# A four-layer decoder step on one core: cache copies issued from ScalarE, key and value tiles in another ring, and a scheduler with other DMA durations

## The chip, the cores and the metric

The kernel runs on one core of one Trainium2 chip. The core's engines are PE (TensorE), ACT (ScalarE), DVE (VectorE) and POOL (GpSimd), each with an instruction queue that is worked off in order, and SP (SyncE), whose queue here only starts transfers; the transfers of all queues run on the core's 16 DMA engines. The metric is the device time of one execution in microseconds; three runs of the kernel before gave 2403.86, 2408.07 and 2417.21 us.

## What is computed

The reference is one inference step of a trunk of four layers, for a prompt of 1024 tokens and a sample of 8 sequences with 4 tokens each. Layers are A (gated short convolution), B (native sparse attention), C (RG-LRU) and A again, each followed by a LayerNorm of `ALPHA * x + mixer(x)`. What bears on the change:

```
def short_conv_mixer(x, buf, w_in, conv_w, w_out):          # layers A
    h, b_gate, c_gate, z = jnp.split(x @ w_in, 4, axis=-1)
    conv, new_buf = causal_dwconv(c_gate * h, buf, conv_w)
    return (jax.nn.silu(z) * b_gate * conv) @ w_out, new_buf

def nsa_mixer(x, past_rows, win_buf, w_in, w_cmp, w_out):   # layer B
    kv = proj[..., D_ATT:D_ATT + n_kvcols].reshape(bsz, t_len, 6, N_KV, HEAD_DIM)
    rows, win_new = kv[:, :, :4], kv[:, :, 4:]
    full = jnp.concatenate([past_rows, rows], axis=1)        # past_rows: 4096 cached rows per sequence
    kv_c = jnp.einsum('bnjcgd,cjgd->bncgd', blocks, w_cmp)   # compressed keys and values, 32 rows to 1
    all_win = jnp.concatenate([win_buf, win_new], axis=1)
    return y, rows, all_win[:, all_win.shape[1] - keep:]     # the last 512 sliding-window rows
```

So the sliding-window output of the sample is, per sequence, rows 4 to 511 of the cached window (508 rows of 1 KB) followed by the 4 new rows: the first part is a plain copy from one DRAM tensor to another, with nothing computed.

## The kernel before

Activations lie feature by token: 8 tiles of 128 features by 1056 tokens (1024 of the prompt, 32 of the sample). A float32 value is kept as a rounded high part and a low remainder, and a product is three matmuls, so one **dense step** (`dense`, L629: one 128-feature output tile, 352 tokens) is 8 x 3 = 24 matmuls of 352 columns into one PSUM bank of the ring "mm" (5 banks). The text calls U[c] the c-th of the eight tiles, from the ring "big", that hold a mixer's output for the out projection.

**First layer** (`layer_a`, L952): 8 channels of 4 x 3 dense steps, 96 in all. For each channel, w = 0 gives h (copied to SBUF by ACT), w = 2 the gate product (DVE), w = 3 the SiLU factor (ACT, DVE), and w = 1 the convolution and the split into U[c] (DVE, ACT). Beside it runs layer B's **compression** of the cache (`compress`, L1296), 64 side steps: POOL gathers 1 MB of cached rows into a tile of "big", SP writes its selection half to the scratch tensor `raw` (two transfers of 256 KB), DVE or POOL multiplies the other half by weights (ring of one tile, reloaded from `in_b_w_cmp` every 8 steps), and DVE sums into one accumulator. Gather n waits for sum n - 3 (`GAHEAD`). Side steps are written out between the dense steps at a rate `RATE`, 0.7 per dense step (`share`, L610); the sums end in `kcd`.

**Out projection** (`out_phase`, L685): 24 dense steps that contract over all of U[0..7], LayerNorm in two rounds through DRAM (`dd`), new activations X.

**Layer B** (`b_project`, L1400): keys and values of 128 tokens at a time in two halves, in groups of four token tiles; each PSUM result is copied by ACT into a tile `kv` of the ring "c" (8 tiles), which also carries the tiles of the LayerNorm that is still running. Its rows are stored by SP, its keys transposed by PE and split by `put_k` (L1426), whose low part for g = 1 goes to DRAM (`kl1`). Then **decode** (`decode`, L1647) for the sample: 36 units of cached keys, fetched from `raw`; in between, `decode_select` for sequence pairs 1 to 3, begun at the units in `SELT`, reads `kcd` into a tile "sel". Then attention of the prompt (`prompt_attention`), with a plan of its own, the out projection, **layer C** (`layer_c`, L1084) and the **last layer** (`layer_a` again, without side steps) with `final_phase`.

**What sets the order.** All parts but the prompt's attention are recorded as steps and laid out by a planner (`Rec.lay`, L378): it simulates the five engines with costs per operation, takes the ready step with the earliest due time, and hands out the tiles of a ring in the order in which the program names them. A transfer costs SP 100 ns, its bytes run over one bus at 360 bytes per ns, and it lands 2000 ns later. The order so found is issued as it stands for four of the engines:

```
with self.tc.manual_schedule(engines={E.PE, E.Activation, E.DVE, E.Pool}):
```

SP is not among them (L485): its queue is ordered by the framework, by the data that a transfer depends on. The copy of the sliding-window rows is written in layer C (`gate_out`, L1189) with a planner's key `("z", c)`, which is no data; its source and destination are DRAM tensors that nothing else writes at these places:

```
nc.sync.dma_start(win_s[c, 0:508, :], cache[c, 4:512, :], rk=[("z", c)])
```

Of the kernel before, what the change touches and what calls it, by code (L numbers as in the profile page):

```python
# [240 lines left out]
class Rec:  # L241
# [136 lines left out]
    def lay(self):  # L378
# [9 lines left out]
        free = {e: 0.0 for e in self.ENGINES}  # L388
# [34 lines left out]
        order, bus, table = [], 0.0, None  # L423
        while True:
            best = None
            for e in self.ENGINES:
                if able[e]:
                    s = free[e]
                elif pend[e]:
                    s = max(free[e], pend[e][0][0])  # L430
# [6 lines left out]
            s, e = best  # L437
            while pend[e] and pend[e][0][0] <= s:
                _, i, o = heapq.heappop(pend[e])
                heapq.heappush(able[e], (o.due, i, o))  # L440
            o = heapq.heappop(able[e])[2]
# [6 lines left out]
            if e == "SP":  # L448
                free[e] = s + 100
                bus = max(bus, s + 100) + o.size / 360  # L450
                o.end = bus + 2000
            else:
                free[e] = o.end = s + cost
                if o.size:
                    bus = max(bus, o.end) + o.size / 360
                    o.end = bus + 2000
# [42 lines left out]
class Trunk:  # L499
# [452 lines left out]
    def layer_a(self, pm, a, X, lp, side=None, nxt=()):  # L952
        nc, io = self.nc, self.io
        stt = nc.vector.scalar_tensor_tensor
        win = io["a_w_in"][a]
        U = [None] * NCH
        SC = lp.tile([P, NCH, 36 if self.later else 18], F32, name="SC")
        todo = [(w, c) for c in range(NCH) for w in (0, 2, 3, 1)]
# [13 lines left out]
        for c in range(NCH):  # L972
            g = self.wsl(1074)
# [3 lines left out]
            W, hs, th = {}, {}, {}  # L977

            def step(w, j):
# [5 lines left out]
                ps = self.mm(pm)[:, 0:TC]  # L985
                self.dense(ps, W[w], X, j)
                if w == 0:
                    hs[j] = self.ct(TC)
                    nc.scalar.copy(hs[j], ps)
                elif w == 2:  # L990
# [8 lines left out]
                else:  # L999
# [4 lines left out]
                    o = j * TC  # L1004
# [79 lines left out]
    def layer_c(self, pm, X, lp):  # L1084
        nc, io = self.nc, self.io
# [103 lines left out]
        def gate_out(c):  # L1189
            h2, i = H[c // 2], c % 2  # L1190
            W = take(("z", c))
            u = self.view2(self.big(F32R))
            U[c] = u
            for j in range(3):
                sl = slice(j * TC, (j + 1) * TC)
                ps = self.mm(pm)[:, 0:TC]
                self.dense(ps, W, X, j)
                th = self.ct(TC)
                nc.scalar.activation(th, ps, AF.Tanh, scale=0.5)
                stt(out=th, in0=th, scalar=1.0, in1=ps, op0=ALU.add, op1=ALU.mult)  # L1200
                stt(out=th, in0=th, scalar=0.5, in1=h2[:, i, sl], op0=ALU.mult, op1=ALU.mult, wk=[("z", c)])
                self.split(u[:, 0, sl], u[:, 1, sl], th, "act", "pool")

            nc.sync.dma_start(win_s[c, 0:508, :], cache[c, 4:512, :], rk=[("z", c)])
        UC, GT, WA, H = {}, {}, {}, {}
        todo = []
        for x in ORDER_C.split():
            c = int(x[1])
# [9 lines left out]
        def take(key):  # L1218
# [5 lines left out]
            return self.pre.pop(key)  # L1224
        win_s = io["o_nsa_win_sample"][0].rearrange("b t c g d -> b t (c g d)")
        cache = io["cache_nsa_win"][0].rearrange("b t c g d -> b t (c g d)")
        for x in ORDER_C.split():
# [172 lines left out]
    def b_project(self, pm, X, bs, ds):  # L1400
# [25 lines left out]
        def put_k(br, ps, g0, n):  # L1426


            for g in range(2):
                kd = K[br]  # L1430
# [12 lines left out]
        for half in range(2):  # L1443
# [8 lines left out]
            for g4 in ((0, 1, 2) if half == 0 else (2, 0, 1)):  # L1452
                tts = range(4 * g4, min(4 * g4 + 4, 9))
                kn = []
                if half == 1 and g4 == 0:
                    side = self.decode_prepare(pm, q2, self.decode_gates(pm, GS, ds), KN, VN, ds)
                for tt in tts:
# [9 lines left out]
                    next(side, None)  # L1467
                    kv = self.ct(nw)
                    if half == 0:
# [763 lines left out]
OUTS = ((0, 0), (0, 1), (1, 0), (1, 1))  # L2233
RATE = 0.7
GAHEAD = 3
# [18 lines left out]
SEL0 = 1  # L2254
SELT = (3, 9, 18)
DSH = dict(sel=7.1, kin=-11.8, begin=-11.6, keys=2.2, score=-10.9, turn=30.4, pv=-26.1, vin=-88.9, first=-37.1, vals=-23.0,
# [191 lines left out]
```

## Time and profile before

| | |
|---|---|
| median of 3 runs | 2408.07 us (2403.86 to 2417.21) |
| profiled execution | 2407.38 us, of which the trace's span is 2405.1 us |
| PE busy | 2303.5 us of the span |
| DVE, ACT, POOL busy | 1573.5, 1197.4, 963.3 us |
| moved by DMA | 320.34 MB, mean 133 GB/s |
| mean granted clock of PE | 0.979 of full speed |

The profile is one execution. Its page gives busy time by engine and in 40 slices of the span; the windows give the same for any stretch, with the count of instructions, so that a stretch in which PE ran slowly shows by fewer matmuls. Waits are put down to the instruction whose semaphore came last. Most instructions carry the line of the recording helper (L310), so they are told apart by the tiles that they write and read: "mm<-x,w" is a dense step on activations, "mm<-big,w" one on U. SP's instructions show when a transfer is started, not when it lands.

### The profile page before, as it was taken

What the parts mean: (1) busy time and instruction counts of PE and PEld (TensorE: products, weight loads), DVE (VectorE), ACT (ScalarE), POOL (GpSimd) and SP (SyncE); (2) the same over time, 40 slices, a digit from 0 to 9 for tenths busy, and PEclk for the clock granted to TensorE, in tenths of its full rate; (3) what the DMA queues carried; (4) which work ended last, traced back from release to release, by engine and by line L of the source; (5) the groups of instructions that cost most, each with busy time, mean ns of one, the idle gap of its engine ahead of it and who ended that gap; (6) DMA issues with size and microseconds to landing.
All of it is one profiled execution on the core that took longest, in us unless ns stands there. A gap on an engine that the chain in (4) does not pass through costs nothing. (4 is left out here: it accounts for less than half of the span.)

```text
span 2405.1 us, 41388 instructions
## 1 busy us (share of the span) xinstructions
PE 2303.5 (96%) x14801; PEld 2233.7 (93%) x14801; DVE 1573.5 (65%) x3686; ACT 1197.4 (50%) x2753; POOL 963.3 (40%) x1070
## 2 busy tenths in 40 slices
PE   8999999897989989999999999999999999999996
PEld 8999998796888879999999998999999999999996
DVE  5776675565348876777777776798875753333336
ACT  3111121234438777888888883378873442222233
POOL 3454543313137855565555663233464320000230
PEclk9999999998999989999999999999999999999998
DMA  8999998438356751111111243341114321111012
GB/s 274 344 350 328 305 293 276 130 124 278 107 163 224 270 193 52 46 41 44 51 40 44 73 137 100 119 138 53 36 46 124 111 62 53 44 45 53 27 55 73
DMA packets 334642, 320.34 MB, mean 133 GB/s; under 512 B 19462, under 2 KB 301542, under 8 KB 324964
## 3 DMA queue, kind: packets, MB, share of 16 engines
q1 hardware_dynamic: 325220, 250.58, 33.9%
q0 software_dynamic: 9216, 67.11, 7.6%
q8 instruction: 117, 1.92, 0.3%
q14 instruction: 89, 0.73, 0.1%
HBM read 237.31 MB, written 84.48 MB: 134 GB/s over the span
## 5 line engine op out<-in xcount | busy, mean ns | idle before, releaser
L310 PE MATMUL mm<-x,w 128*128 128x352 f32 x5760 | 943.8, 325 | 19.0 <-DVE ws L310 10.5
L310 PEld LDWEIGHTS mm<-x,w 128*128 128x128 f32 x5760 | 933.4, 190 | 24.0 <-DVE ws L310 8.1
L310 PE MATMUL mm<-big,w 128*128 128x352 f32 x2208 | 379.5, 326 | 12.0 <-ACT big L310 9.6
L310 PEld LDWEIGHTS mm<-big,w 128*128 128x128 f32 x2208 | 358.0, 189 | 15.8 <-ACT big L310 9.9
L310 POOL TENSOR_TENSOR w<-ws,w 128x1024 fp32r<-128x1024 f32 (+1 forms) x43 | 105.9, 2462 | 419.2 <-ACT w L310 416.9
L1993 DVE TENSOR_TENSOR c<-T,c 128x512 fp32r<-128x512 f32 (+1 forms) x320 | 204.7, 648 | 49.5 <-ACT c L1989 44.8
L1989 ACT CAST c<-T 128x512 fp32r<-128x512 f32 (+1 forms) x320 | 174.5, 552 | 59.3 <-PE T L1985 38.3
L310 ACT CAST w<-ws 128x1024 fp32r<-128x1024 f32 (+2 forms) x116 | 120.3, 1038 | 161.8 <-PE mm L310 116.4
L641 PE MATMUL D<-x,w 128*128 128x352 f32 x1008 | 195.4, 330 | 2.2 <-DVE big L2120 2.2
L1895 PE MATMUL A<-big 128*128 128x320 f32 (+11 forms) x832 | 181.7, 334 | 3.4 <-DVE ast L1920 1.6
L2000 PE MATMUL O<-c,big 128*128 128x256 f32 x1056 | 180.4, 291 | 0.5 <-ACT c L1989 0.2
L310 POOL TENSOR_TENSOR big<-big,ws 128x1024 f32<-128x1024 f32 (+1 forms) x38 | 90.1, 2370 | 208.1 <-DMA big<-in_cache_nsa_kv,idx 101.7
L641 PEld LDWEIGHTS D<-x,w 128*128 128x128 f32 x1008 | 159.8, 188 | 5.7 <-DVE big L2120 3.5
L310 ACT CAST big<-aux 128x352 fp32r<-128x352 f32 (+3 forms) x116 | 45.4, 402 | 236.6 <-DVE aux L310 163.9
L310 DVE TENSOR_TENSOR w<-ws,w 128x1024 fp32r<-128x1024 f32 (+2 forms) x73 | 92.7, 1269 | 100.9 <-ACT w L310 100.3
L310 DVE TENSOR_TENSOR big<-big 128x256 f32<-128x256 f32 (+3 forms) x204 | 140.8, 711 | 24.1 <-POOL big L310 22.5
L2000 PEld LDWEIGHTS O<-c,big 128*128 128x128 f32 x1056 | 147.2, 189 | 2.6 <-DVE c L1993 0.7
L1953 POOL TENSOR_SCALAR pr<-pr,G,ast 128x32 f32<-128x32 f32 (+6 forms) x192 | 126.4, 672 | 47.0 <-DVE ast L1964 38.6
L1895 PEld LDWEIGHTS A<-big 128*128 128x128 f32 x832 | 134.4, 193 | 10.2 <-PE A L1895 2.2
L310 ACT ACTIVATE aux<-ws,PT 128x352 f32<-128x352 f32 (+2 forms) x72 | 42.5, 596 | 172.6 <-DVE ws L310 170.9
L1949 ACT ACTIVATE pr<-pr,ast 128x32 f32<-128x32 f32 (+6 forms) x192 | 118.4, 619 | 17.9 <-DVE ast L1920 16.8
L310 DVE SCALAR_TENSOR_TENSOR c<-c,mm 128x352 f32<-128x352 f32 x125 | 64.2, 516 | 88.6 <-ACT c L310 46.2
(286 smaller groups left out, 4031.1 us busy)
## 6 DMA issues: line engine op xcount, KB each, us to landing
ws<-in_a_w_in SPq DMA_DIRECT2D x64, 512.0 KB
raw<-big SPq DMA_DIRECT2D x128, 256.0 KB
big<-raw SPq DMA_DIRECT2D x128, 256.0 KB
c<-dd SPq DMA_DIRECT2D x48, 176.0 KB
xs<-x SPq DMA_DIRECT2D x24, 352.0 KB
x<-xs SPq DMA_DIRECT2D x8, 1056.0 KB
ws<-in_a_w_out SPq DMA_DIRECT2D x16, 512.0 KB
ws<-in_c_w_in SPq DMA_DIRECT2D x16, 512.0 KB
```

The source lines that it names most:

```text
L310: getattr(real, name)(*[f(x) for x in a], **{q: f(x) for q, x in k.items()})
L641: self.nc.tensor.matmul(ps, a, b, start=n == 0, stop=n == 23 and last)
L1895: nc.tensor.matmul(o, q[:, hl, i * P:(i + 1) * P], k, start=m == 0, stop=m == 1)
L1949: nc.scalar.activation(S[:, a:a + m], S[:, a:a + m], AF.Exp, bias=st[:, k:k + 1], scale=-1.0, accum_out=st[:, 3 + k:4 + k])
L1953: nc.gpsimd.tensor_scalar(S[:, a:a + m], S[:, a:a + m], G[:, i, 16 * k + h:16 * k + h + 1], st[:, 6 + k:7 + k], op0=ALU.mult, op1=ALU.mult)
L1989: nc.scalar.copy(x["H"][:, 0:n], x["tp"][:, 0:n])
L1993: nc.vector.tensor_sub(x["L"][:, 0:n], x["tp"][:, 0:n], x["H"][:, 0:n].bitcast(F32))
L2000: nc.tensor.matmul(O, v, M[:, y * P:(y + 2) * P], start=done[0] == 0, stop=done[0] == total - 1)
```

## The change

1. The planner charges SP 400 ns per transfer instead of 100 and lets the bus carry 330 bytes per ns instead of 360, for SP's transfers and POOL's gathers.
2. The eight copies of sliding-window rows are no longer issued by SP from layer C's code. ACT issues them in the last layer, one per channel, behind the copy of the third h tile (w = 0, j = 2). ACT's order is laid out by hand, so they stay there.
3. In `b_project` each group of up to four `kv` tiles takes one slot of the ring "big" (18 slots) in place of up to four tiles of the ring "c".
4. `put_k` handles g = 1, whose low part goes through a "c" tile to DRAM, before g = 0.
5. `RATE` goes from 0.7 to 0.75, and `SELT` from (3, 9, 18) to (5, 10, 18).

The diff:

```diff
--- before.py
+++ after.py
@@ -446,13 +446,13 @@
                     cost += 1283
                 table = f
             if e == "SP":
-                free[e] = s + 100
-                bus = max(bus, s + 100) + o.size / 360
+                free[e] = s + 400
+                bus = max(bus, s + 400) + o.size / 330
                 o.end = bus + 2000
             else:
                 free[e] = o.end = s + cost
                 if o.size:
-                    bus = max(bus, o.end) + o.size / 360
+                    bus = max(bus, o.end) + o.size / 330
                     o.end = bus + 2000
             order.append(o)
             o.start = s
@@ -954,6 +954,7 @@
         stt = nc.vector.scalar_tensor_tensor
         win = io["a_w_in"][a]
         U = [None] * NCH
+        win_s, win_c = (io[x][0].rearrange("b t c g d -> b t (c g d)") for x in ("o_nsa_win_sample", "cache_nsa_win"))
         SC = lp.tile([P, NCH, 36 if self.later else 18], F32, name="SC")
         todo = [(w, c) for c in range(NCH) for w in (0, 2, 3, 1)]
         wkey = lambda x: ("a", a) + x
@@ -986,7 +987,10 @@
                 self.dense(ps, W[w], X, j)
                 if w == 0:
                     hs[j] = self.ct(TC)
-                    nc.scalar.copy(hs[j], ps)
+                    nc.scalar.copy(hs[j], ps, wk=[("h", a, c)] if j == 2 else [])
+                    if j == 2 and side is None:
+
+                        nc.scalar.dma_start(win_s[c, 0:508, :], win_c[c, 4:512, :], rk=[("h", a, c)])
                 elif w == 2:
                     nc.vector.tensor_mul(g[:, 2 + j * TC:2 + j * TC + np_], ps[:, 0:np_], hs[j][:, 0:np_])
                     if j == 2:
@@ -1200,8 +1204,6 @@
                 stt(out=th, in0=th, scalar=1.0, in1=ps, op0=ALU.add, op1=ALU.mult)
                 stt(out=th, in0=th, scalar=0.5, in1=h2[:, i, sl], op0=ALU.mult, op1=ALU.mult, wk=[("z", c)])
                 self.split(u[:, 0, sl], u[:, 1, sl], th, "act", "pool")
-
-            nc.sync.dma_start(win_s[c, 0:508, :], cache[c, 4:512, :], rk=[("z", c)])
         UC, GT, WA, H = {}, {}, {}, {}
         todo = []
         for x in ORDER_C.split():
@@ -1222,8 +1224,6 @@
             for k in todo[i + 1:i + 2]:
                 fetch(k)
             return self.pre.pop(key)
-        win_s = io["o_nsa_win_sample"][0].rearrange("b t c g d -> b t (c g d)")
-        cache = io["cache_nsa_win"][0].rearrange("b t c g d -> b t (c g d)")
         for x in ORDER_C.split():
             c = int(x[1])
             if x[0] == "u":
@@ -1426,7 +1426,7 @@
         def put_k(br, ps, g0, n):
 
 
-            for g in range(2):
+            for g in (1, 0):
                 kd = K[br]
                 r0, r1 = slice(64 * g, 64 * g + 64), slice(64 - 64 * g, 128 - 64 * g)
                 sl = slice(g0, g0 + n)
@@ -1452,6 +1452,7 @@
             for g4 in ((0, 1, 2) if half == 0 else (2, 0, 1)):
                 tts = range(4 * g4, min(4 * g4 + 4, 9))
                 kn = []
+                four = self.big()
                 if half == 1 and g4 == 0:
                     side = self.decode_prepare(pm, q2, self.decode_gates(pm, GS, ds), KN, VN, ds)
                 for tt in tts:
@@ -1465,7 +1466,7 @@
                             nc.tensor.matmul(ps, a, b, start=n == 0, stop=n == 23)
                             n += 1
                     next(side, None)
-                    kv = self.ct(nw)
+                    kv = four[:, len(kn) * nw:(len(kn) + 1) * nw]
                     if half == 0:
                         nc.scalar.copy(kv, ps)
                     else:
@@ -2231,7 +2232,7 @@
 FOFF = 7
 OUT0, OUTD, OUT1, OUTE = 119.07, 2.4, 114, 0.993
 OUTS = ((0, 0), (0, 1), (1, 0), (1, 1))
-RATE = 0.7
+RATE = 0.75
 GAHEAD = 3
 ORDER_C = "u101 u001 u12 u02 u2 g0 u5 z0 u3 g1 u4 g2 z1 z2 g3 u6 g4 u7 g5 z4 z3 g6 z6 z5 g7 z7"
 NLO = (((2, 5, 6, 7), (3, 4, 6), (0, 5)), ((6, 7), (0, 5, 7), (2, 7)), ((2, 4, 6, 7), (1, 2, 6), (0, 1, 2, 3, 6, 7)))
@@ -2252,7 +2253,7 @@
 TAILV = 39
 VLO = 0b10010010
 SEL0 = 1
-SELT = (3, 9, 18)
+SELT = (5, 10, 18)
 DSH = dict(sel=7.1, kin=-11.8, begin=-11.6, keys=2.2, score=-10.9, turn=30.4, pv=-26.1, vin=-88.9, first=-37.1, vals=-23.0,
        fin=17.8, fold=-41.1, weights=-59.0, exps=-96.3)
 DN = 3, 3, 3, 1
```

Since the planner's durations and rates are changed, the order of all parts is laid out anew, but for the prompt's attention. Three places:

The copies. SP in the first layer before (`raw` and `ws` are the compression's writes and the layer's weights), and ACT in the last layer after the change.

```order
L310 DMA raw<-big 128x4x128 x2
L310 DMA out_nsa_win_sample<-in_cache_nsa_win 16x8128
L310 DMA ws<-in_a_w_in 128x8x128
L310 DMA raw<-big 128x4x128 x8
L310 DMA ws<-in_a_w_in 128x8x128
L310 DMA out_nsa_win_sample<-in_cache_nsa_win 16x8128
L310 DMA ws<-in_a_w_in 128x8x128
L310 DMA raw<-big 128x4x128 x4
L310 DMA ws<-in_a_w_in 128x8x128
```

```order
L310 CAST x<-ws 128x352
L310 ACTIVATE c<-mm 128x352
L310 CAST x<-ws 128x352
L310 ACTIVATE aux<-ws,PT 128x352 x2
L310 CAST w<-ws 128x1024
L310 COPY c<-mm 128x352
L310 DMA out_nsa_win_sample<-in_cache_nsa_win 16x8128
L310 CAST w<-ws 128x1024
L310 ACTIVATE aux<-ws,PT 128x368
```

Two of the eight copies stood in these rows of SP, though the code names them in layer C; the first of ACT's eight now stands behind a "c<-mm" copy of the last layer.

The start of the first out projection on PE, before and after the change. Before, big_3805 is U[7] (big_708 is U[0]); after, big_3734 and big_3932 are U[6] and U[7], and each mm is one of the five banks.

```order
L310 MATMUL mm_3841<-big_2486,w_3633 128x352 x3
L310 MATMUL mm_3841<-big_2930,w_3633 128x352 x3
L310 MATMUL mm_3841<-big_3387,w_3633 128x352 x3
L310 MATMUL mm_3841<-big_3805,w_3633 128x352 x3
L310 MATMUL mm_3875<-big_708,w_3633 128x352 x3
L310 MATMUL mm_3875<-big_1175,w_3633 128x352 x3
L310 MATMUL mm_3875<-big_1588,w_3633 128x352 x3
L310 MATMUL mm_3875<-big_2032,w_3633 128x352 x3
```

```order
L310 MATMUL mm_3885<-big_2684,w_3697 128x352 x3
L310 MATMUL mm_3885<-big_3221,w_3697 128x352 x3
L310 MATMUL mm_3907<-big_710,w_3697 128x352 x3
L310 MATMUL mm_3907<-big_1207,w_3697 128x352 x3
L310 MATMUL mm_3907<-big_1705,w_3697 128x352 x3
L310 MATMUL mm_3907<-big_2179,w_3697 128x352 x3
L310 MATMUL mm_3907<-big_2684,w_3697 128x352 x3
L310 MATMUL mm_3907<-big_3221,w_3697 128x352 x3
L310 MATMUL mm_3807<-big_3734,w_3589 128x352 x3
L310 MATMUL mm_3807<-big_3932,w_3589 128x352 x3
L310 MATMUL mm_3885<-big_3734,w_3697 128x352 x3
L310 MATMUL mm_3885<-big_3932,w_3697 128x352 x3
```

Before, one bank takes its 21 matmuls on U[0] to U[6] and then needs U[7]. Now five banks take 18 matmuls each on U[0] to U[5] (the rows show the fourth from its fifth row and the fifth) before the first of them needs U[6] and U[7]. On DVE the first piece of U[7] stands behind the 63rd of the 64 sums in both orders, and the next one behind the pair sums of the 64th gather. Of the sums before, many stand later than they did: sum 41 behind 49 of DVE's 72 dense-step results of the layer, where it stood behind 45.

The first key and value copies on ACT (COPY c<-mm and big<-mm), before and after. ACTIVATE c<-c,PT and CAST x<-c are the LayerNorm that is still running, CAST big<-ws the split of the query weights.

```order
L310 ACTIVATE c<-c,PT 128x352 x2
L310 CAST x<-c 128x352 x2
L310 CAST big<-ws 128x1024
L310 COPY c<-mm 128x384
L310 ACTIVATE c<-c,PT 128x352
L310 COPY c<-mm 128x384
L310 CAST x<-c 128x352
L310 COPY c<-mm 128x384
L310 ACTIVATE c<-c,PT 128x352
L310 CAST x<-c 128x352
L310 COPY c<-mm 128x384
```

```order
L310 ACTIVATE c<-c,PT 128x352 x2
L310 CAST big<-ws 128x1024
L310 CAST x<-c 128x352 x2
L310 ACTIVATE c<-c,PT 128x352 x2
L310 CAST x<-c 128x352
L310 COPY big<-mm 128x384 x4
L310 CAST x<-c 128x352
L310 ACTIVATE c<-c,PT 128x352 x2
L310 CAST x<-c 128x352 x2
L310 CAST big<-ws 128x1024
```

Four copies that stood apart, behind the split of the last query weight, now stand together ahead of it.

## Rows read from the trace of the kernel before

**Rows 1.** Page, parts 1 and 2: busy us (share), and DMA share in 40 slices.

```profile
PE 2303.5 (96%) x14801; PEld 2233.7 (93%) x14801; DVE 1573.5 (65%) x3686; ACT 1197.4 (50%) x2753; POOL 963.3 (40%) x1070
...
DMA  8999998438356751111111243341114321111012
```

**Rows 2.** Windows by stage: us, busy (x count) per engine, PE clock, DMA share, GB/s.

```profile
36.00:180.00 144.00, 144.00 (x898) 144.00 (x898) 105.33 (x163) 29.43 (x52) 75.97 (x44) 1.00 1.01 344
...
180.00:444.00 264.00, 236.34 (x1380) 231.42 (x1379) 172.89 (x295) 45.54 (x84) 114.88 (x64) 0.94 0.91 293
...
536.00:600.00 64.00, 49.16 (x235) 43.26 (x233) 40.33 (x73) 32.57 (x61) 24.39 (x23) 0.81 0.85 290
...
690.00:712.00 22.00, 15.20 (x88) 13.32 (x89) 12.38 (x35) 9.83 (x23) 5.59 (x8) 0.84 0.71 220
...
1440.00:1950.00 510.00, 497.88 (x3123) 490.81 (x3122) 389.21 (x801) 298.81 (x546) 201.28 (x172) 0.99 0.29 88
1950.00:2340.00 390.00, 390.00 (x2444) 389.56 (x2443) 139.81 (x270) 89.34 (x166) 37.96 (x32) 1.00 0.17 49
```

**Rows 3.** Windows, one slice of the first layer, same columns.

```profile
300.00:312.00 12.00, 9.33 (x41) 9.08 (x40) 10.15 (x23) 2.71 (x5) 4.28 (x3) 0.72 0.99 325
```

**Rows 4.** Waits of PE, 180 to 445 us: total us, times, longest us.

```profile
PE mm L310 <- DVE ws L310: 10.5, 5, 3.1
PE mm L310 <- ACT big L310: 9.6, 1, 9.6
```

**Rows 5.** Waits of DVE, 180 to 445 us, same columns.

```profile
DVE big L310 <- DMA ws<-in_b_w_cmp: 38.7, 5, 10.8
DVE big L310 <- DMA big<-in_cache_nsa_kv,idx: 24.7, 7, 6.4
```

**Rows 6.** Instructions on the copied rows' output: ns min/median/max, first and last start.

```profile
L310 SPq DMA_DIRECT2D out_nsa_win_sample<-in_cache_nsa_win x8: 529/1098/4707, 24.3 to 224.9; - x8
```

**Rows 7.** Timeline, 408 to 446 us: start, us, engine, operation [idle before <- releaser].

```profile
418.28 3.53 PE L310 MATMUL mm<-big,w 128*128 128x352 f32 x21
...
425.59 1.22 DVE L310 TENSOR_TENSOR big<-big,ws 128x1024 f32<-128x1024 f32 x1 [6.31 <-DMA big<-in_cache_nsa_kv,idx]
...
428.07 2.43 POOL L310 TENSOR_TENSOR big<-big,ws 128x1024 f32<-128x1024 f32 x1 [3.92 <-DMA big<-in_cache_nsa_kv,idx]
...
430.86 0.45 ACT L310 CAST big<-aux 128x352 fp32r<-128x352 f32 x1 [21.55 <-DMA raw<-big]
...
431.36 5.03 PE L310 MATMUL mm<-big,w 128*128 128x352 f32 x15 [9.56 <-ACT big L310]
```

**Rows 8.** Waits of PE, 536 to 712 us, columns as in group 4.

```profile
PE mm L310 <- ACT c L310: 7.0, 1, 7.0
PE aux L310 <- DMA sel<-kcd: 6.8, 1, 6.8
PE aux L310 <- POOL c L310: 2.5, 2, 2.2
```

**Rows 9.** Timeline of ACT, 540 to 592 us.

```profile
577.28 1.04 ACT L310 CAST big<-ws 128x1024 fp32r<-128x1024 f32 x1 [0.88 <-DMA ws<-in_b_w_in]
578.23 0.47 ACT L310 COPY c<-mm 128x384 f32<-128x384 f32 x1
...
582.44 0.48 ACT L310 COPY c<-mm 128x384 f32<-128x384 f32 x1 [1.52 <-DMA xd<-c]
```

**Rows 10.** Timeline of PE, 536 to 606 us.

```profile
578.76 2.29 PE L310 MATMUL mm<-w,x 128*128 128x384 f32 x6 [6.97 <-ACT c L310]
```

**Rows 11.** Timeline, 690 to 712 us.

```profile
697.60 0.32 SPq L310 DMA_DIRECT2D sel<-kcd  x1
...
701.12 0.66 PE L310 MATMUL aux<-idf,sel 128*128 128x128 f32 x2 [6.80 <-DMA sel<-kcd]
```

**Rows 12.** Windows, ACT alone in the last layer: us, busy (x count), clock, DMA share, GB/s.

```profile
1950.00:2290.00 340.00, 72.57 (x126) 1.00 0.17 47
```

**Rows 13.** Groups by line, ACT, 1560 to 1760 us: count, busy us, mean ns.

```profile
L310 ACT ACT_TABLE_LOAD x27 | 34.6, 1283 | 1.7 <-PE mm L310 1.3
```

## The prediction

> **What bounds the kernel now.** I read the page first: PE is busy for 2303.5 us, 96% of the span [rows 1], so all that a new order can win lies in some 100 us in which PE stands still, and in what its clock costs after each stop. The same page shows the DMA engines at 8 tenths or more for the first seven slices, some 420 us, and far below that in the last layer. So I took windows by stage [rows 2]. From 36 to 180 us PE never stops: 898 matmuls in 144 us, 0.160 us each, at a granted clock of 1.00, with DMA at a share of 1.01 and 344 GB/s. From 180 to 444 us DMA is at 0.91 and 293 GB/s, and PE is idle for 27.7 us. The idle time is not the whole loss: at the earlier pace 264 us hold 1646 matmuls, and 1380 are there; the 266 that are missing are worth 42.7 us. The other 15 us are slow matmuls: in a slice in which PE was idle for 2.7 of 12 us, the mean granted clock is 0.72, a mix of its two levels (1.2 and 2.4 GHz), and 41 matmuls are done [rows 3]. So every stop is paid about one and a half times.
>
> Who stops PE there? Mostly DVE, late with evicting a bank, and once ACT, for 9.6 us [rows 4]. Neither is short of time; DVE sits in its queue behind steps of the compression whose data have not landed: 38.7 us for the weights, 24.7 us for gathers [rows 5]. The timeline shows the end of it [rows 7]: PE does 21 matmuls of the out projection from 418.28 us and then waits until 431.36 us for ACT's cast into U[7]; ACT waits for DVE, and DVE and POOL wait for the last gathers, which they begin to use at 425.59 and 428.07 us. The first layer ends with the transfers, not with PE. What else loses much are two places: 536 to 600 us (14.8 us idle, clock 0.81) and 690 to 712 us (6.8 us idle, clock 0.84) [rows 2]. The last layer has no idle time on PE at all.
>
> **The copies.** The code puts them into layer C, but SP starts them between 24.3 and 224.9 us [rows 6], within the stretch in which DMA is full. They are 8 x 508 KB, 4.16 MB. From 180 to 444 us the engines moved 293 GB/s at a share of 0.91, thus 322 GB/s when busy: 12.9 us of DMA time that the first layer no longer pays.
>
> The Trainium skill (DMA: Bandwidth & Descriptors, section "Issuing engines are not separate DMA queues") says that transfers of all issuing engines run on the same 16 DMA engines, and that issuing from another engine saves sequencer time alone. It speaks against any gain from ACT's queue as such, and by it this item would be worth nothing if the copies stayed in the first layer. They do not stay there: the order of ACT has them in the last layer.
>
> There they compete with 47 GB/s at a share of 0.17 [rows 12] and with a PE that never waits. ACT pays the starts: 8 x 1.1 us at SP's median, 8 x 4.7 us at its longest [rows 6], against 267 us in which ACT is idle there. Behind a start stand casts of weights and activations, and the h tile just copied is read by DVE only after the next dense steps. Cost 0; without that cover it would be 9 to 38 us.
>
> **The first layer.** U[7] stays behind the last gathers in DVE's order, so its time moves with the transfers. Two things bring them forward: the 12.9 us, and some of the time in which DMA stood partly idle (9% of 264 us, 24 us). With the slower bus in the plan, DVE's sums stand behind more dense steps, so DVE should block less on data not landed, and side steps are written out sooner. I take a quarter, 6 us. U[7] is then ready at 431.4 - 18.9 = 412.5 us. And PE will have done 90 matmuls instead of 21 by then, because five banks now go ahead on U[0] to U[5]: 69 x 0.160 = 11.0 us. It can: 418.3 us less the some 30 us lost before is 388, and 14.4 us for the 90 make 403. So this stage gains 18.9 + 11.0 = 30 us, and PE still waits some 10 us at its end. The ends: 11 us if the transfers end when they did, 43 us if the whole loss goes. What is late next is U[7] still.
>
> **Keys and values.** After 571 us five banks are full and PE waits 7.0 us for ACT's first copy into a "c" tile [rows 8]. That copy stands behind a cast that waited for its weight (577.28), and is done only then (578.23); the third waits for a store to release its tile (582.44) [rows 9]; PE goes on with six matmuls in 2.29 us [rows 10] and waits 2.2 us more for POOL's products, which need "c" tiles as well [rows 8]. With tiles of "big" the four copies stand together and ahead of that cast: the first is about 2.4 us earlier (the cast, 1.04 us, its wait, 0.88 us, and one cast of X, 0.48 us), and the later ones wait for no store. Of 9.2 us idle and some 3 us of slow matmuls I take 7 back. Ends: 0 (the tiles wait for slots of "big" instead) and 12. Groups take slots one after another as stores land, but five banks let PE run ahead.
>
> **Decode.** PE waits 6.8 us for "sel" [rows 8], whose transfer starts at 697.60 and is needed by PE at 694.3; PE goes on at 701.12 [rows 11]. Starting the first selection at unit 5 puts another unit's transposes and scores on PE ahead of it, and g = 1 first in `put_k` frees the last "c" tile sooner. I take 5 us. Ends: 8 (wait and slow clock) and -3: the preloaded keys of units 0 and 1 (1 MB, 3.3 us at 322 GB/s) now find a slot only when layer B ends, since the key and value tiles hold one, and may be late.
>
> **The rest.** From 1440 to 1950 us PE is idle for 12.1 us [rows 2]; the order there is new, with two more table loads on ACT, 1.28 us each [rows 13]. Nothing says which way: 0, with 4 us to either side. The attention of the prompt and the tail keep their order: 0.
>
> **The sum.** 30 + 7 + 5 = 42 us off the profiled execution: 2407.4 - 42 = 2365.4 us. The median of the runs is 0.7 us above that execution, so I predict **2366 us**.
>
> **Rivals.**
> - *The transfers end when they did.* The gathers are held by sums (n - 3) and by slots, not by bandwidth alone, and 24 us of slack did not help them before; the copies may only have filled holes. Then PE gains 11 us in the first layer and the other two terms: 2407.4 - 11 - 12 = 2384 us. Against it: at a share of 1.01 to 180 us, with most of the copies in it, bytes do set the pace.
> - *The whole loss goes.* 293 GB/s x 264 us are 77.4 MB, and some 76 without what of the copies falls into it; at the 344 GB/s of the first stretch they take 221 us, and the last gather lands at about 401 us, before PE has used up its 403. Then 43 + 12 = 55 us go: 2352 us. For it: 344 GB/s was held for 144 us. Against it: DVE's and POOL's shares in the chain don't shrink. The Trainium skill (same page, section "Where 436 GB/s comes from") gives a core's share of HBM as about 358 GB/s, by which bytes would not bind this stage; the windows show at most 344 over a long stretch, so the trace only half agrees.
> - *The new order holds the gathers back.* Sums stand up to 6 of 72 results later, which is 8 of 96 dense steps, 8 x 24 x 0.160 = 31 us; gather n waits for sum n - 3, so DMA may idle in the middle of the layer and pay at its end. U[7] would be ready at 431.4 - 12.9 + 31 = 449.5 us instead of 412.5, PE's loss there 37 us more than forecast: 2403 us. It turns to slower from about 454 us on, and if DVE, blocked by late sums, stops PE by another 10.5 us as it does now [rows 4], which one and a half times is 16 us, it is 2419 us. Against it: a later sum is also a sum that waits less, and DMA had a queue to work off.
>
> **How the numbers follow.** Forecast 0.60 (2355 to 2378, by the ends of the terms taken together loosely), transfers unmoved 0.20 (2384), whole loss 0.12 (2352), gathers held back 0.08 (2403 to 2419). Differences under 0.5%, 12 us, can hardly be told from none by these runs. Faster than 2396 us: the first three, less what may go wrong elsewhere, 0.87; within 12 us: 0.09; slower 0.04. The range of 8 in 10 takes in the first three cases with some room on the slow side: 2345 to 2397 us.
>
> **What would show it.** Right: from 180 us on the stops "mm <- DVE ws" are mostly gone; the kcd write and U[7] come 15 to 20 us sooner; a wait of some 10 us on U[7] stays, behind about 90 matmuls; the 7.0 and 6.8 us waits shrink to 3 or less; the copies start in the last layer with PE at full pace there. Wrong: DMA's share well under 0.9 between 200 and 400 us, U[7] no sooner than 428 us, or new waits for "big" slots in layer B.

## The result and the profile after

The changed kernel takes 2385.28 us (median of 4 runs, 2383.58 to 2388.22); the kernel before, run on the same chip beside it, 2412.64 us (4 runs, 2403.86 to 2417.5). The ratio is **0.9892, with a 95% interval of 0.9856 to 0.9928**: 26 us or 1.1% faster. That is the right side, and inside the range of 2345 to 2397 us, but it is not the forecast's 2366 us: it is the first rival, "the transfers end when they did", which gave 2384 us. That the two times agree to 1 us is in part luck: with a fourth run the median of the kernel before lies 4.6 us above the one that the forecast started from. As a gain, the rival has 23 us; measured are 26 us by the ratio and 20.4 us in the profiled executions.

The profiled execution has a span of 2384.7 us, 20.4 us less than before. Page, parts 1 and 2, answering to [rows 1]:

```profile
PE 2293.3 (96%) x14801; PEld 2223.1 (93%) x14801; DVE 1592.3 (67%) x3686; ACT 1198.2 (50%) x2755; POOL 958.2 (40%) x1070
...
DMA  7899989547268651111111234331114222122112
```

PE's busy time fell by 10 us with as many matmuls, since fewer ran at the lower clock: the mean granted clock is 0.986 of full speed, before it was 0.979. The windows by stage, columns as in [rows 2]:

```profile
36.00:180.00 144.00, 143.62 (x894) 143.33 (x893) 109.83 (x155) 29.13 (x51) 72.70 (x44) 1.00 0.93 308
180.00:444.00 264.00, 243.02 (x1469) 240.17 (x1468) 195.50 (x312) 48.17 (x89) 118.47 (x66) 0.97 0.93 300
...
1950.00:2340.00 390.00, 390.00 (x2448) 389.45 (x2448) 139.85 (x272) 92.62 (x178) 36.61 (x30) 1.00 0.19 53
```

Beside [rows 2]: in the second window 89 more matmuls are done and PE is idle for 21.0 us instead of 27.7. The stops "mm <- DVE ws" (10.5 us before) are gone, but between 36 and 445 us PE waits 9.2 us for DVE's "c" tiles in their place. And in the first window DMA moved 308 GB/s where it had moved 344, so the bytes of the copies are gone there and nothing has taken their place. The end of the first layer, PE's timeline, answering to [rows 7]:

```profile
405.72 11.76 PE L310 MATMUL mm<-big,w 128*128 128x352 f32 x72
419.05 3.67 PE L310 MATMUL mm<-big,w 128*128 128x352 f32 x21 [1.57 <-DVE c L310]
432.15 6.89 PE L310 MATMUL mm<-big,w 128*128 128x352 f32 x27 [9.43 <-ACT big L310]
```

93 matmuls of the out projection stand ahead of the wait, where 21 stood. But PE goes on at 432.15 us, and before it did at 431.36: U[7] has not come sooner at all. What ACT's cast into U[7] waited for, and where the compression ends (SP's write of `kcd`):

```profile
431.65 1.14 ACT L310 CAST big<-aux 128x352 fp32r<-128x352 f32 x3 [17.85 <-DMA raw<-big]
...
434.78 0.34 SPq L310 DMA_DIRECT2D kcd<-big  x1
```

The `kcd` write had started at 434.03 us before, so the compression has not ended sooner either. And the trace puts ACT's wait down to the landing of a raw write that SP started at about 426 us, when a late page had been gathered; DVE's last result for these casts had been ready at 422.49 us. As far as this releaser shows, U[7] waits for its tile: a slot of "big" with a gathered page in it that is still being written out. The same row of the kernel before also names a raw write [rows 7].

The copies did go where the order put them. Instructions on the copied rows' output, answering to [rows 6]:

```profile
L310 ACTq DMA_DIRECT2D out_nsa_win_sample<-in_cache_nsa_win x8: 517/517/647, 1925.5 to 2230.1; - x8
```

In the last layer PE is busy for all of 390 us, as before. Waits of PE from 536 to 712 us, answering to [rows 8]:

```profile
PE mm L310 <- ACT big L310: 5.3, 1, 5.3
PE aux L310 <- DVE c L310: 2.4, 2, 1.3
...
PE aux L310 <- DMA sel<-kcd: 0.6, 1, 0.6
```

**Where the 20.4 us of span came from**, by the same instruction of PE (or DVE) in both traces:

| stage, to its end mark | before | after | gain |
|---|---|---|---|
| first layer and out projection, to layer B's first matmul | 536.75 | 523.50 | 13.25 |
| layer B's projections, to the first cached key | 688.43 | 667.73 | 7.45 |
| decode, to the prompt's attention | 863.55 | 839.84 | 3.0 |
| attention itself, to its last matmul `A<-big` | 1448.9 | 1425.1 | 0.1 |
| layer C to the final norm's first `fsum` | 2291.7 | 2271.3 | -3.4 |

The forecast had 30, 7, 5, 0 and 0.

### The profile page after: what moved, and what is told of

It is laid out like the page before. It is cut to its first block, busy times and chain, and to the rows that moved or that the text cites. A ratio compares the mean times of both kernels' runs of the same rounds, so it can differ in the third digit from the quotient of the medians.

```text
span 2384.7 us, 41361 instructions
## 1 busy us (share of the span) xinstructions
PE 2293.3 (96%) x14801; PEld 2223.1 (93%) x14801; DVE 1592.3 (67%) x3686; ACT 1198.2 (50%) x2755; POOL 958.2 (40%) x1070
## 3 DMA queue, kind: packets, MB, share of 16 engines
q10 hardware_dynamic: 256, 4.16, 0.6%
## 5 line engine op out<-in xcount | busy, mean ns | idle before, releaser
L310 PEld LDWEIGHTS mm<-big,w 128*128 128x128 f32 x2208 | 357.8, 189 | 20.4 <-ACT big L310 9.7
L310 DVE TENSOR_TENSOR big<-big 128x256 f32<-128x256 f32 (+3 forms) x204 | 176.1, 883 | 20.0 <-POOL big L310 18.0
L310 POOL TENSOR_TENSOR big<-big,ws 128x1024 f32<-128x1024 f32 (+1 forms) x38 | 92.6, 2438 | 197.3 <-DMA ws<-in_b_w_cmp 68.2
L310 POOL TENSOR_TENSOR big<-big 128x512 fp32r<-128x512 f32 (+2 forms) x74 | 86.4, 1185 | 111.9 <-DVE big L310 83.2
```

Of the source, the lines that this page charges most:

```text
L310: getattr(real, name)(*[f(x) for x in a], **{q: f(x) for q, x in k.items()})
```

## The experiments

The first four take the change apart. The theory on record was "bytes": the first layer ends when its transfers have ended, so fewer bytes or a fuller bus bring U[7] forward. The rival was "holes": the copies only filled time in which the bus had nothing else to do, and order sets the end.

**The copies alone.** The kernel before with the copies issued by ACT in the last layer, nothing else:

```diff
-            nc.sync.dma_start(win_s[c, 0:508, :], cache[c, 4:512, :], rk=[("z", c)])
+                    if j == 2 and side is None:
+                        nc.scalar.dma_start(win_s[c, 0:508, :], win_c[c, 4:512, :], rk=[("h", a, c)])
```

> The kernel before with one part of the change: ScalarE issues the eight copies of sliding-window rows in the last layer; durations, rates, rings as before. Theory 'bytes' (the last gathers land when the first layer's DMA bytes are through): 12.9 us fewer, so ScalarE's cast into U[7] moves from 431 to about 418 us and the time falls by 13 to 20 us. Theory 'order' (gather n is held by sum n - 3, by the one tile of compression weights and by the planned places of the sums; the copies only filled holes): U[7] within 4 us of 431, time within 5 us of before.

2411.56 us, ratio 1.0007 (0.9997 to 1.0016): nothing gained. Its first window and PE's timeline:

```profile
36.00:180.00 144.00, 139.79 (x857) 138.96 (x857) 95.98 (x154) 27.51 (x48) 74.46 (x42) 0.99 0.91 302
```

```profile
429.53 3.53 PE L310 MATMUL mm<-big,w 128*128 128x352 f32 x21
440.44 5.03 PE L310 MATMUL mm<-big,w 128*128 128x352 f32 x15 [7.38 <-ACT big L310]
```

4.16 MB less to move, and U[7] is 9 us later in the profiled execution, which is the slowest of the eleven runs (2421.88 us, 10.3 us above the median), so only that U[7] came no sooner can be taken from it. The orders of PE, DVE, ACT and POOL are those of the kernel before, but for the eight copies; SP's is not. The framework lays it out, and without the copies it also put some writes of raw pages ahead of weight loads that they had stood behind.

**The DMA durations alone.** The kernel before with SP at 400 ns and the bus at 330 bytes per ns:

```diff
-                free[e] = s + 100
-                bus = max(bus, s + 100) + o.size / 360
+                free[e] = s + 400
+                bus = max(bus, s + 400) + o.size / 330
```

> The kernel before with SP at 400 ns per transfer and the bus at 330 bytes per ns in the planner, nothing else. The copies stay in the first layer. Bytes: U[7] stays at 431 us or later, and only PE's order can gain (up to 11 us at the start of the out projection), so 0 to 11 us faster. Order: U[7] moves by more than 4 us with the plan, either way; if the plan alone cured VectorE's waits, the time would fall by 10 to 20 us.

2392.97 us, ratio 0.9937 (0.9921 to 0.9954), about 15 us. Here 93 matmuls are ahead as well, from 391.28 us on, and PE then waits 19.38 us for U[7] at 426.53. The wait for the key copies (7.1 us) and the one for "sel" (7.0 us) are still there.

**Keys and values alone.** The kernel before with the `kv` tiles in "big" and g = 1 first:

```diff
+                four = self.big()
...
-                    kv = self.ct(nw)
+                    kv = four[:, len(kn) * nw:(len(kn) + 1) * nw]
```

> The kernel before with key and value tiles in the large ring and the other order in put_k, nothing else. Both theories: the first layer unchanged, layer B's first half 7 us shorter (the 7.0 us wait shrinks to under 3), the wait for sel at the start of decode shorter by 2 us or unchanged, time 5 to 10 us under before. If slots of the large ring are what the copies then wait for, no gain.

2400.86 us, ratio 0.996 (0.9943 to 0.9976), some 10 us. The wait for "sel" is gone with the old `SELT`, and PE waits 1.7 us for the key copies instead of 7.0.

**All but the copies.** The changed kernel, with the copies on SP from layer C's code again:

```diff
-                        nc.scalar.dma_start(win_s[c, 0:508, :], win_c[c, 4:512, :], rk=[("h", a, c)])
+            nc.sync.dma_start(win_s[c, 0:508, :], cache[c, 4:512, :], rk=[("z", c)])
```

> The changed kernel with the copies back in layer C's code on SP, where they are started early. Bytes: U[7] comes 13 us later than the changed kernel's 432 us, at about 445 us, and the time is 13 us above the changed kernel, about 11 us under before. Order: U[7] within 4 us of 432, time within 4 us of the changed kernel.

2380.48 us, ratio 0.9879 (0.9863 to 0.9896). That overlaps the changed kernel's interval, so the copies' move neither helps nor can be shown to hurt. The gain of the whole change is thus that of the new order and of the key and value tiles, some 15 and 10 us by themselves. PE's timeline:

```profile
400.60 15.10 PE L310 MATMUL mm<-big,w 128*128 128x352 f32 x93
424.19 6.77 PE L310 MATMUL mm<-big,w 128*128 128x352 f32 x27 [8.49 <-ACT big L310]
```

With all the copies' bytes in the first layer U[7] is 8 us earlier than without them, and the write of `kcd` too (426.82 us). "Bytes" as I had used it has fallen: these bytes don't set the end. What holds the first layer, then? In one place of the changed kernel DMA is busy for little more than a third of the time:

```profile
84.00:96.00 12.00, 12.00 (x76) 12.00 (x75) 6.76 (x14) 4.39 (x7) 0.00 (x0) 1.00 1.05 337
96.00:108.00 12.00, 12.00 (x77) 12.00 (x76) 8.72 (x13) 1.91 (x4) 6.15 (x4) 1.00 0.37 101
```

Its SP queue at that place (start, us from the first start of the row to the end of its last):

```profile
88.26 2.75 SPq L310 DMA_DIRECT2D raw<-big  x1
91.12 0.64 SPq L310 DMA_DIRECT2D ws<-in_a_w_in  x1
91.80 2.93 SPq L310 DMA_DIRECT2D raw<-big  x3
94.83 1.55 SPq L310 DMA_DIRECT2D ws<-in_b_w_cmp  x2
110.83 0.92 SPq L310 DMA_DIRECT2D raw<-big  x2
```

And POOL's timeline:

```profile
101.38 3.44 POOL L310 TENSOR_TENSOR big<-big,ws 128x1024 f32<-128x1024 f32 x1 [19.85 <-DMA ws<-in_b_w_cmp]
104.97 1.25 POOL L315 DMA_INDIRECT big<-in_cache_nsa_kv,idx  x1 [0.16 <-POOL big L310]
```

SP starts the compression weights only at 94.83 us, behind raw writes, though their tile was free: the last product with the old weights had ended on POOL at 80.4 us. POOL waits 19.85 us for them; the next gather stands behind its product in POOL's queue and starts at 104.97 us; and SP's next raw write waits for that gather until 110.83 us, with weight loads behind it. Between 36 and 445 us POOL waited 68.2 us and DVE 34.7 us for these weights. Three runs on the changed kernel asked which link of this loop counts. None of them settles it, since each also gave all queues a new order.

**A longer lead for the gathers** (`GAHEAD` 3 to 6):

> The changed kernel with each page gather waiting for the sum six pages back in place of three. Theory 'sums': the first layer's last tile waits on gathers that are let go too late; then DVE's and SP's waits for gathered pages shrink (SP's were 104.5 us in 180 to 445), U[7] comes 5 us or more before 432 and the time falls to 2380 or less. Theory 'weight tile': the gathers stand because the slots they fill are not read, for want of the compression weights; then U[7] stays within 4 us of 432 and the time within 4 us of 2385. Theory 'bytes' says the same as 'weight tile' here: no byte is changed.

2385.9 us, ratio 0.992 (0.9903 to 0.9936). U[7] came at 424.67 us, as "sums" wants, but the time did not move, as the other theories want. The gathers did not end sooner: the write of `kcd` starts at 434.81 us, in the changed kernel at 434.78. In this order the trace puts the wait of ACT's cast into U[7] down to DVE and no longer to a raw write, so U[7] came sooner by itself, and PE, which did 792 matmuls from 36 to 180 us where the changed kernel did 894, then waited for it only 1.3 us. So the run neither supports the loop nor rules it out.

**Two tiles for the compression weights** (`k.apart(1)` to `k.apart(2)`):

> The changed kernel with two tiles in place of one set apart for the compression weights (the layer's weight rows have one tile less). Theory 'weight tile': POOL's 68 us and DVE's 35 us of waits for the compression weights between 36 and 445 fall to under 25 us together, the dip of the DMA share at 96 to 108 us goes, U[7] comes 6 us or more before 432, and the time falls to 2379 or less. Theory 'sums' or 'bytes': those waits fall too, but U[7] stays within 3 us of 432, or comes later since the layer's own weights have a tile less, and the time is 2383 or more.

2406.93 us, ratio 0.9998 (0.9985 to 1.0012): all of the change's gain is gone. The waits for the compression weights vanished, and U[7] came at 426.66 us, but the write of `kcd` at 435.59 us, no sooner than in the changed kernel. And the layers' own weights have a tile less. POOL and PE in this run, 36 to 445 and 500 to 640 us:

```profile
POOL w L310 <- ACT w L310: 69.4, 10, 23.3
```

```profile
PE mm L310 <- ACT w L310: 11.5, 2, 10.2
```

POOL's 68 us of waiting only changed its name, and layer B's first matmul came at 549.84 us, 26 us later than in the changed kernel: PE waited 10.2 us for its weight, and 15 us for POOL, DVE and ACT in the LayerNorm ahead of it, where the changed kernel had no wait.

**Compression weights from ACT's queue**, into the same tile:

```diff
-                nc.sync.dma_start(w[:, :, c * P:(c + 1) * P], a.unsqueeze(0)...
+                nc.scalar.dma_start(w[:, :, c * P:(c + 1) * P], a.unsqueeze(0)...
```

> The changed kernel with the sixteen loads of the compression weights issued from ScalarE's queue in place of SP's, into the same single tile. If the loads are late because they stand behind the writes of raw pages on SP, the waits for them (68 us on POOL, 35 us on DVE) fall by half or more and U[7] comes 4 us or more before 432, with the time at 2381 or less. If they are late because the single tile comes free late, the waits stay within 25% and the time within 4 us of 2385.

2400.65 us, ratio 0.9969 (0.9954 to 0.9984), slower than the changed kernel by more than was expected. POOL waits 67.7 us for the weights, DVE 54.8, together 19% more than in the changed kernel: by the waits this is the second outcome, that the single tile comes free late, but the time is 15 us above the 2385 that goes with it. At the place shown above ACT starts the load at 94.11 us, behind a cast that had waited 9.69 us for a weight of the layer. Another queue with waits in it does not make the loads early, and how much of these waits is the queue and how much the single tile stays open.

**The rate put back** (`RATE` 0.7):

> The changed kernel with the side work's rate put back from 0.75 to 0.7. If the rate is what ends the product for the block selection's wait for the compressed keys (6.8 us before, 0.6 us after), the wait returns to 5 us or more and the time goes up by 4 to 7 us over the changed kernel's 2385. If the order of the first layer under the new DMA durations does that already, the wait stays under 2 us and the time stays within 3 us of it.

2388.5 us, ratio 0.9917 (0.9901 to 0.9934); "sel" is waited for 0.9 us. The rate isn't what ended that wait.

**SP in the planner's order.** This run asks the question directly. The changed kernel, copies on ACT, with SP's order held by the planner like that of the other four engines (in `Rec.issue`):

```diff
-        with self.tc.manual_schedule(engines={E.PE, E.Activation, E.DVE, E.Pool}):
+        with self.tc.manual_schedule(engines={E.PE, E.Activation, E.DVE, E.Pool, E.SP}):
```

> The changed kernel with SP's instructions issued in the planner's order too (the framework's own scheduler orders SP otherwise). Theory 'order of SP': the planner puts the compression weights' two loads and the weight rows of the layer where its own sums need them, POOL's and DVE's waits for the compression weights (103 us together) fall by half, U[7] comes at 426 or before and the time at 2380 or less. Theory 'bytes': the same bytes in another order end when they did, U[7] 429 to 435, time within 4 us of 2385. A third outcome is that waits on SP for gathers now stand in front of ready weights and U[7] comes later than 436.

**2369.1 us, ratio 0.9834 (0.9817 to 0.985)**, some 14 us below the changed kernel, whose interval lies just above this one, and the lowest ratio of the study. U[7] and the time are as the theory "order of SP" has them. The four other engines run the changed kernel's order, instruction for instruction, so SP's order is all that differs. PE's timeline, and the windows:

```profile
391.86 15.10 PE L310 MATMUL mm<-big,w 128*128 128x352 f32 x93
416.33 6.17 PE L310 MATMUL mm<-big,w 128*128 128x352 f32 x27 [9.36 <-ACT big L310]
```

```profile
96.00:108.00 12.00, 12.00 (x77) 12.00 (x76) 11.40 (x13) 1.87 (x3) 9.39 (x6) 1.00 1.01 329
...
36.00:180.00 144.00, 144.00 (x898) 144.00 (x898) 111.82 (x161) 29.95 (x53) 76.27 (x45) 1.00 0.96 322
180.00:444.00 264.00, 254.64 (x1573) 253.24 (x1573) 198.89 (x321) 54.65 (x97) 125.64 (x72) 0.98 0.92 301
```

U[7] and the write of `kcd` (418.96 us) both come 15.8 us sooner, and the hole at 96 us is filled. Layer B's first matmul comes 16.55 us sooner, at 506.95 us, and the two spans differ by 18.2 us: nearly all of the gain lies ahead of layer B. SP's queue there starts the compression weights at 88.33 us:

```profile
86.77 1.46 SPq L310 DMA_DIRECT2D ws<-in_a_w_in  x1
88.33 3.77 SPq L310 DMA_DIRECT2D ws<-in_b_w_cmp  x2
92.20 3.15 SPq L310 DMA_DIRECT2D raw<-big  x4
95.47 1.21 SPq L310 DMA_DIRECT2D ws<-in_a_w_in  x1
```

SP's waits for gathered pages from 36 to 445 us, of the changed kernel, then of the one without the copies' move, then of this one:

```profile
SPq L310 <- DMA big<-in_cache_nsa_kv,idx: 151.2, 30, 14.4
```

```profile
SPq L310 <- DMA big<-in_cache_nsa_kv,idx: 117.8, 28, 12.2
```

```profile
SPq L310 <- DMA big<-in_cache_nsa_kv,idx: 72.8, 24, 9.7
SPq L310 <- POOL w L310: 46.3, 8, 7.5
```

These three kernels have the same order on the four other engines (but for the copies), U[7] at 432.2, 424.2 and 416.3 us, and the write of `kcd` at 434.8, 426.8 and 419.0. SP's order sets the end of the compression. Which link of the loop it does this by is not shown. SP waits about as long in all in the three kernels (185, 178 and 181 us); in the planned order it waits less for gathers and more for weight tiles that POOL releases (46.3 us, 2.6 in the changed kernel). And the waits of POOL and DVE for the compression weights fell from 103 to 57 us, a little less than the half that was expected, but they are 61 us in the kernel without the copies' move, with U[7] 8 us later.

**Fewer bytes of another kind.** The kernel before with half of the raw writes left out:

```diff
-                for i in range(2):
+                for i in range(1):
                     nc.sync.dma_start(self.raw[b, :, jg, i], ...)
```

> The kernel before with half of the raw pages' writes left out (the second block of 128 columns is not written, and layer B's decoding reads the first in its place): 32 writes of 256 KB less, 8.4 MB, with the copies where they were. At 344 GB/s these bytes are 24.4 us. Theory 'bytes': U[7] comes 15 us or more before 431.4, and the time falls by 10 us or more from the kernel before. Theory 'holes and order': the transfers already stand idle for want of gathers and slots, U[7] stays at 423 or later and the time within 8 us of the kernel before.

2383.96 us, ratio 0.9902 (0.9883 to 0.9922), by the ratio 24 us less, as much as the bytes at 344 GB/s; the write of `kcd` starts at 409.9 us instead of 434.0, and ACT's cast into U[7] at 403.0 instead of 430.9. This is the outcome of "bytes": unlike the copies, these writes hold a slot of "big" until they have landed, and the next load stands behind them. But the run cannot tell how much of it is bytes and how much is 32 instructions less in a queue that blocks: SP still waits 217.7 us for gathers (206.7 before), DMA's share from 180 to 444 us is 0.76 (0.91 before), and the orders of SP, POOL and DVE are all new, since the planner reckons with the writes.

**The longer lead with the copies on SP** (`GAHEAD` 6, then 4, on the kernel without the copies' move):

> The changed kernel with the eight copies back on SP's queue, and each page gather waiting for the sum six pages back in place of three. With three, the copies on SP gave 2380.5 us and U[7] at 424.2; six alone, with the copies on ScalarE, brought U[7] to 424.7. If the two gains add up, U[7] comes at 418 or before and the time at 2375 or less. If both only fill the same idle stretches of the transfers, U[7] stays between 421 and 428 and the time within 4 us of 2380.

> The same with four pages in place of six. If the order of transfers alone decides, with no trend in the number of pages, this stands as far from 2380 as any new order did in the runs so far (within 8 us either way, U[7] between 420 and 433); if gathers let go sooner help by their number, it stands between 2380 and the kernel with six.

2377.53 us, 0.9865 (0.9847 to 0.9884), and 2372.22 us, 0.9854 (0.9834 to 0.9873); U[7] at 422.10 and 415.86. Both intervals overlap that of the 0.9879 of three pages, so neither a gain nor a trend is shown. With six pages the two shifts don't add up, as the second outcome has it. With four, neither outcome came true as stated: U[7] came before 420 us, and the time lies below that of six pages. But the write of `kcd` starts at 426.66 us with four pages, as with three (426.82), and at 432.08 with six: the gathers ended no sooner, U[7] only no longer hung on the last of them. The interval of four pages also overlaps that of SP's planned order, so which of the two is faster is not shown.

## Why the prediction was right in sign and 19 us off

**The bound.** Right: the first layer ends with its transfers, not with PE. In every profile with 93 matmuls ahead PE then waited, 8.49 to 19.38 us, for the cast into U[7]. By which way was misread: "ACT waits for DVE" stands beside a row that names a raw write, and in these five profiles too the cast was let go by the landing of a raw write and not by DVE's order.

**The step that failed** is in the term of the first layer: "Two things bring them forward: the 12.9 us, and some of the time in which DMA stood partly idle", so that U[7] is ready at 412.5 us. It was ready at 432.15. I took the share of 0.91 to 1.01 to mean that bytes set the pace, and took the bytes away. But a share near 1 over 144 us hid a loop: raw writes on SP wait for gathers, gathers wait for products on POOL, products wait for weights, and the weights are in SP's queue behind raw writes. The trace of the changed kernel shows the loop at one place (the share of 0.37 at 96 us), and the runs show that SP's order sets its end; that every part of it counts is argued. A copy that hangs on nothing takes the room that such a loop leaves: the copies alone gave a ratio of 1.0007, their first window fell from a share of 1.01 to 0.91, and nothing else used the room. SP's order was read for the copies alone, not for what else had changed places in it. The run with SP's order planned gives 416.33 us for U[7] and 2369.1 us, near the 412.5 and 2366 that the step wanted, but by another way than fewer bytes; a planned order with the copies' bytes in the first layer was not run.

**More matmuls ahead**: right. 72 more instead of the 69 of the forecast, 11.5 us at 0.160; the stage gained 13.25 us. With U[7] 0.8 us later, another 2.5 us came between U[7] and layer B: before, PE waited there 2.1 us for DVE's "c" tile, and in the changed kernel it does not wait at all.

**Keys and values**: 7.45 us where 7 were forecast, by another way. The wait for the key copies went from 7.0 to 5.3 us only, not to 3 or less. Over the stage PE was idle for 14.8 us before and 11.2 after, and the mean granted clock rose from 0.92 to 0.98, worth the other 3.8 us: POOL's 2.5 us and DVE's 2.3 us of the old order are almost gone. The tiles alone took 1.9 us off this stage, the durations alone 4.3 with the 7.1 us wait in place.

**Decode**: the wait went from 6.8 to 0.6 us, the stage gained 3.0 us against 5: small waits on POOL and DVE came up in its place. Keys and values alone end that wait, with the old `SELT`; that `SELT` adds to it is not shown.

**The rest**: -3.4 us where 0 was taken, within the 4 us given. From the attention's last start to the first `fsum` the four kernels with the old durations take 842.0 to 844.2 us, the ten with the new ones 845.9 to 848.4: the new order of layer C costs a little.

**The copies in the last layer**: cost 0, as predicted.

**The rivals.** "The transfers end when they did" named the mechanism (copies that fill holes, gathers held by sums and slots) but not SP's order, and it had the smaller chance on the strength of the share of 1.01 alone. "The new order holds the gathers back" did not happen as stated: U[7] was 0.8 us later, not 18.

## What to carry to other kernels

A transfer that nothing waits for and that waits for nothing can cost a full queue nothing that shows, as the copies did here: before counting its bytes as a gain, look for what the queue's head waits for, and whether the load that would free it stands in the same queue. A busy share near 1 of the DMA engines is not yet a bound by bytes; here the same bytes on SP in another order ended 16 us sooner. An event that stands for "the transfers have ended" has to be checked too: in the four runs with a longer lead or a second weight tile U[7] came sooner while the write of `kcd` did not. When four engines' orders are planned and one is left to another scheduler, an edit can reshuffle that one, as the copies alone did, and a small edit then shows the new order and not its own worth.

## What was not expected

- Removing eight free-standing copies let U[7] come 9 us later in the profile with nothing else changed on four engines (431.36 to 440.44 us), while the median of the time stayed; that profile is of the slowest run.
- The start of the same 508 KB copy took 517 ns at the median on ACT's queue in the quiet last layer, and 1098 ns, up to 4707, on SP's in the full first layer [rows 6].
- A tile taken from the layers' weights to hold more of the compression's cost as much as the whole change had gained (0.9998 against 0.9892).
